# Attention trunk on one core: the input rows ahead of the weights, and a written-out order for the prologue

## The chip, the cores and the metric

The kernel runs on one NeuronCore of one Trainium2 chip, as one launch. The metric is device time in microseconds (us), the median over several executions. 0.2% of it is 3.0 us.

## The reference

A two-layer decoder trunk over 1040 tokens (16 learned meta tokens, then 1024 rows of x), width 1024, float32. Each layer does this:

```python
u = rms_norm(h, norm_g)
proj = jnp.einsum('bld,dp->blp', u, w_in)      # 4104 columns
dq, dk, dv, dz, fq, fk, fv, fz, f_logit = jnp.split(proj, split_points, axis=-1)
q1, q2 = diff_qk(dq); k1, k2 = diff_qk(dk)     # with rotary embedding
p = probs(qa, k1) - lam * probs(qc, k2)        # 4 differential heads, causal
...                                            # 8 forgetting heads with a decay term
mixed = jnp.concatenate([o_a * silu(dz), o_b * silu(fz)], axis=-1)
h = h + jnp.einsum('blm,md->bld', mixed, w_out)
```

After the second layer a last RMSNorm is applied and the meta tokens are dropped.

## The kernel before

Every large product is made of three matmuls: each operand is split into a high and a low part (`whi`, `wlo` for weights, `XTh`, `XTl` for the transposed input), and hi x hi, lo x hi and hi x lo are accumulated in PSUM.

**The prologue** (lines 947 to 996) makes `XTh` and `XTl` for layer 0. A few matmuls without use (`WARM = 20`, line 951, each run as two instructions) go first. Then x comes in as eight blocks of 128 rows (512 KB each), the meta tokens as a ninth block of 16 rows, and the norm's weights `gb` as a broadcast of 512 KB; all of them on SP's DMA queue (lines 956 to 964). With `W0 = 0` the loop also calls `load_w` right after its first block: the weights of the first key projection (128 columns, 512 KB, two DMAs of 256 KB) go out on ACT's DMA queue (`WQ0`, line 308), and POOL splits them (lines 325 and 328).

The nine blocks are normed in three groups of three (`GRPS`, line 969). For a group, ACT squares and sums each block (line 260), DVE makes the reciprocal roots of the three sums together (lines 235 to 248) and scales each block (line 271). Then `put_ut` (line 274) transposes each block on PE in two halves (line 286), ACT copies a half into `XTh` (line 296), and DVE subtracts to make `XTl` (line 297). The first group is block 0 (meta) with blocks 1 and 2; the key projection's first chunk of 272 tokens needs that group alone, the second chunk of 384 the second group, and the third chunk the third.

`prefetch(0, PF0)` with `PF0 = "qv"` then asks for the first query projection's weights (two DMAs of 256 KB on ACT's queue, `WQ1`) and for the value weights of units 0 and 1 together with the forget weights (`load_v01`, line 362). The rotary tables `cos` and `sin` follow (lines 999 and 1000).

**The projections** of unit 0 (`unit_proj`, line 482) are key, query and value in the text's order. `proj` (line 344) takes one chunk after the other: 24 matmuls over the eight pieces k of the contraction, then the evacuation. After the evacuation of chunk 1 the keys go through the rotary embedding (lines 509 to 514: four DMAs on SP, DVE, POOL, DVE).

**The rest** is eight units of attention in each layer, four differential and four forgetting; the next unit's projections are issued among the attention of the present one. A differential query block copies its low query part into one of `NQZ = 3` zeroed buffers on POOL (`low_queries`, line 673), from which PE reads (line 692).

**What sets the order.** The program is given to a planner (line 1182, `schedule_with_timeline_sim` and `auto_bufs`). It models a timeline, orders each engine's instructions (SP's and ACT's DMA issues too) by when each could be issued and how soon its result is due, and may so leave the order of the text. Each engine then runs its list in order. Where a pool has a number of buffers written out (`STB = 3` for the pool `stk` with the keys, queries and half of the prologue's rows), the planner keeps to it; where there is none (`bufs=None`), it chooses one that the memory has room for.

## Time and profile before

| | |
|---|---|
| median of 3 executions | 1485.57 us (1485.4 to 1487.66) |
| the profiled execution | 1487.34 us |
| its span, first to last instruction | 1485.6 us |
| PE busy with matmuls | 1416.9 us, 95% of the span |
| DVE, ACT, POOL busy | 958.7, 698.6, 619.2 us |
| mean granted TensorE clock | 0.983 |

PE is the TensorE, DVE the VectorE, ACT the ScalarE, POOL the GpSimd, and SP the engine that issues most DMAs; "PEld" is PE's weight load and "q" behind an engine's name its sequencer, which waits and issues. Times in rows are us from the start of the span. In a timeline, a row's two first numbers are the start and the length of a run of like instructions (xN says how many), and what stands in brackets is how long the engine sat idle before it and which event ended that. PEclk is the share of TensorE's full 2.4 GHz that was granted: 0.50 is 1.2 GHz.

### The profile page before, as it was taken

What the parts mean: (1) busy time and instruction counts of PE and PEld (TensorE: products, weight loads), DVE (VectorE), ACT (ScalarE), POOL (GpSimd) and SP (SyncE); (2) the same over time, 40 slices, a digit from 0 to 9 for tenths busy, and PEclk for the clock granted to TensorE, in tenths of its full rate; (3) what the DMA queues carried; (4) which work ended last, traced back from release to release, by engine and by line L of the source; (5) the groups of instructions that cost most, each with busy time, mean ns of one, the idle gap of its engine ahead of it and who ended that gap; (6) DMA issues with size and microseconds to landing.
All of it is one profiled execution on the core that took longest, in us unless ns stands there. A gap on an engine that the chain in (4) does not pass through costs nothing.

```text
span 1485.6 us, 26706 instructions
## 1 busy us (share of the span) xinstructions
PE 1416.9 (95%) x9262; PEld 1350.0 (91%) x9262; DVE 958.7 (65%) x2721; ACT 698.6 (47%) x1729; POOL 619.2 (42%) x1118
## 2 busy tenths in 40 slices
PE   4889989999999999999998989999999999999997
PEld 4888989999999999996888989899999999999886
DVE  4548796867765666655654678677757565655554
ACT  3335554545554555554323455444446455544511
POOL 2616463542435443654015345445424444445400
PEclk7999999999999999999999999999999999999999
DMA  9315240353324234358333142324331323253632
GB/s 193 74 30 73 39 93 16 65 62 69 71 49 71 61 56 82 82 152 200 114 110 75 29 60 48 68 47 64 53 87 29 82 44 80 55 118 91 228 109 91
DMA packets 112215, 119.63 MB, mean 81 GB/s; under 512 B 15376, under 2 KB 92816, under 8 KB 112080
## 3 DMA queue, kind: packets, MB, share of 16 engines
q1 hardware_dynamic: 104592, 104.09, 32.2%
q10 hardware_dynamic: 7488, 13.83, 4.7%
q8 instruction: 73, 1.20, 0.3%
q14 instruction: 62, 0.51, 0.1%
HBM read 70.92 MB, written 21.54 MB: 62 GB/s over the span
## 4 chain that ended last, share of the span: by engine, by line
PE 75%; DVE 7%; DMA 4%; ACT 2%; issue 2%; SPq 1%; POOL 1%; DVEq 0%; ACTq 0%; POOLq 0%
PE pj L352 36%; PE pss L1073 5%; PE pj L1073 5%; PE pss L690 4%; PE pss L692 4%; PE pt L865 4%; PE po L800 3%; PE pj L417 3%; PE po L799 2%; DMA sw<-raw 1%; SPq L137 1%; DVE E L696 1%; PE pt L1073 1%; DVE raw L511 1%; DMA mt<-ms 1%
## 5 line engine op out<-in xcount | busy, mean ns | idle before, releaser
L352 PE MATMUL pj<-XTh,whi 128*128 128x346 f32 (+5 forms) x1392 | 453.8, 328 | 5.0 <-ACT XTh L296 1.9
L352 PE MATMUL pj<-XTh,wlo 128*128 128x346 f32 (+5 forms) x1392 | 452.9, 326 | 1.2 <-POOL wlo L328 1.2
L352 PE MATMUL pj<-XTl,whi 128*128 128x346 f32 (+5 forms) x1392 | 451.8, 325 | 1.1 <-DVE XTl L297 1.1
L352 PEld LDWEIGHTS pj<-XTh,whi 128*128 128x128 f32 x1392 | 264.3, 190 | 9.0 <-POOL whi L325 1.9
L352 PEld LDWEIGHTS pj<-XTh,wlo 128*128 128x128 f32 x1392 | 265.1, 190 | 2.5 <-POOL wlo L328 1.8
L352 PEld LDWEIGHTS pj<-XTl,whi 128*128 128x128 f32 x1392 | 264.8, 190 | 2.3 <-DVE XTl L297 1.7
L696 DVE CUSTOM_DVE_ANT_0 E<-pss,cst 128x346 f32<-128x346 f32 (+6 forms) x384 | 212.0, 558 | 77.0 <-PE pss L692 61.7
L703 ACT ACTIVATE E<-E,cst 128x656 f32<-128x656 f32 (+3 forms) x192 | 172.5, 898 | 141.7 <-DVE cst L696 137.8
L328 POOL TENSOR_TENSOR wlo<-wraw,whi 128x256 fp32r<-128x256 f32 x232 | 182.1, 785 | 16.3 <-PE pt L760 1.3
L774 DVE TENSOR_TENSOR ptl<-pt,pth 128x512 fp32r<-128x512 f32 (+1 forms) x240 | 147.6, 633 | 34.8 <-ACT pth L773 30.7
L690 PE MATMUL pss<-k,qa 128*128 128x400 f32 (+7 forms) x448 | 152.8, 347 | 12.1 <-DVE cst L696 6.9
L773 ACT CAST pth<-pt 128x512 fp32r<-128x512 f32 (+1 forms) x240 | 123.3, 545 | 72.8 <-PE pt L865 30.9
L325 POOL TENSOR_SCALAR whi<-wraw 128x256 fp32r<-128x256 f32 x232 | 101.0, 436 | 116.4 <-DMA wraw<-in_w_in_dram 115.2
L720 POOL TENSOR_SCALAR E<-E,cst 128x400 f32<-128x400 f32 (+2 forms) x96 | 83.7, 873 | 138.2 <-DVE cst L719 127.2
L673 POOL TENSOR_SCALAR XTl<-ql 64x128 fp32r<-64x128 f32 x136 | 53.0, 396 | 151.3 <-PE pss L692 127.3
L690 PEld LDWEIGHTS pss<-k,qa 128*128 128x128 f32 x448 | 84.8, 190 | 16.9 <-DVE cst L696 9.7
L865 PE MATMUL pt<-cst,E 128*128 128x128 f32 x576 | 87.1, 273 | 0.3 <-DVE cst L762 0.3
L799 PE MATMUL po<-pth,V 128*128 128x256 f32 x320 | 82.7, 283 | 0.0
L800 PE MATMUL po<-ptl,V 128*128 128x256 f32 x320 | 82.3, 286 | 0.0
L512 POOL TENSOR_TENSOR sw<-sw,sin 128x694 f32<-128x694 f32 (+5 forms) x32 | 50.6, 1581 | 76.0 <-DMA sw<-raw 63.8
L692 PE MATMUL pss<-k,q 68*128 68x400 f32 (+6 forms) x224 | 71.7, 326 | 0.5 <-DMA qa<-qa 0.5
L692 PE MATMUL pss<-k,XTl 128*128 128x400 f32 (+6 forms) x224 | 71.5, 325 | 0.0
(303 smaller groups left out, 2944.3 us busy)
## 6 DMA issues: line engine op xcount, KB each, us to landing
wraw<-in_w_in_dram SPq DMA_DIRECT2D x244, 128.0 KB
hb<-in_x_dram SPq DMA_DIRECT2D x16, 512.0 KB
wor<-in_w_out_dram SPq DMA_DIRECT2D x64, 128.0 KB
ms<-OT SPq DMA_DIRECT2D x8, 520.0 KB
k<-k ACTq DMA_DIRECT2D x16, 260.0 KB
h<-hb SPq DMA_DIRECT2D x8, 512.0 KB
ms<-OT SPq DMA_DIRECT2D x8, 512.0 KB
hb<-h SPq DMA_DIRECT2D x8, 512.0 KB
```

The source lines that it names most:

```text
L328: nc.gpsimd.tensor_tensor(out=lo, in0=raw, in1=hi.bitcast(F32), op=ALU.subtract)
L352: nc.tensor.matmul(ps[:, :n], lhsT=w, rhs=xx[:, k, t0:t0 + n], start=(cnt == 0), stop=(cnt == 23))
L690: nc.tensor.matmul(ps[:, :nn], lhsT=U.Qa[m][:, t:t + P], rhs=U.K1[m][:, c0:c0 + nn], start=True, stop=False)
L692: nc.tensor.matmul(ps[:, :nn], lhsT=low[m], rhs=U.Kb[m][:, c0:c0 + nn], start=False, stop=True)
L696: nc.vector.tensor_tensor_reduce(out=E[:, c0:c0 + n], in0=ps[:, :n], in1=k, scale=-1.0, scalar=s[:, c - 1:c] if CHN and c else -NEG, op0=A ...
L703: nc.scalar.activation(E[:, :W], E[:, :W], AF.Exp, scale=-1.0, bias=lo, accum_out=s[:, 4:5])
L773: nc.scalar.copy(hi, ps)
L774: nc.vector.tensor_tensor(out=lo, in0=ps, in1=hi.bitcast(F32), op=ALU.subtract)
L799: nc.tensor.matmul(o[:, :256], lhsT=U.V[:, kb, hd, :], rhs=hi, start=False, stop=False)
L800: nc.tensor.matmul(o[:, :256], lhsT=U.V[:, kb, hd, :], rhs=lo, start=False, stop=last)
L865: nc.tensor.transpose(ps[:, (2 * a + b) * P:(2 * a + b + 1) * P], PP[:, k0:k0 + P], ident)
L1073: nc.tensor.matmul(ps, lhsT=xx[:, k, m0:m0 + P], rhs=wo[k][w][:, c], start=(k == 0 and i == 0), stop=(k == KT - 1 and i == 2))
```

## The change

The key weights are loaded after the ninth block (`W0 = 8`), on SP's queue instead of ACT's, in four DMAs of 128 KB instead of two of 256 KB. The query weights go to SP as well (four DMAs of 128 KB through the small `es` buffers), behind the key weights; the tables go behind them, and the value weights behind the tables. `tc.issue_after(ins)` queues what its block holds behind `ins` on the engine of `ins`. With it, the transposes of the first two groups are followed on PE by the key projection's first two chunks, made together: piece k for chunk 0, piece k for chunk 1, then piece k+1 (`both`). The third group's transposes are held back (`late_ut`) and queued behind that pair. The DVE work of the value weights and of `setup_scalars` is queued behind the third group's last subtraction. The useless matmuls ahead become 40 (`WARM`), the zeroed query buffers 2 (`NQZ`), and the pool `stk` has no written-out number of buffers (`STB = 0`).

```diff
--- before.py
+++ after.py
@@ -14,6 +14,9 @@
 F32R = mybir.dt.float32r
 BF16 = mybir.dt.bfloat16
 I32 = mybir.dt.int32
+PE = mybir.EngineType.PE
+SP = mybir.EngineType.SP
+DVE = mybir.EngineType.DVE
 AF = mybir.ActivationFunctionType
 ALU = mybir.AluOpType
 
@@ -36,7 +39,7 @@
 MW = 584
 AHEAD = 3
 XORD = (1, 0, 2, 3, 4, 5, 6, 7, 8)
-W0 = 0
+W0 = 8
 ON_POOL = ()
 SPL_POOL = ()
 GRPS = ((0, 1, 2), (3, 4, 5), (6, 7, 8))
@@ -49,8 +52,8 @@
 ENG = ('g','d')
 WLB = 6
 VPB = 0
-STB = 3
-NQZ = 3
+STB = 0
+NQZ = 2
 PMB = 4
 OTB = 2
 Q2B = 2
@@ -70,14 +73,14 @@
 PQ = 0
 SH = 0
 PP = ()
-WARM = 20
+WARM = 40
 CKB = (0,)
 KR = True
 PG = ()
 AQ = True
 AV = True
-WQ0 = True
-WQ1 = True
+WQ0 = False
+WQ1 = False
 CORD = (1, 0, 2, 3)
 PSB = (0, 0, 0, 0)
 Z_AT = {0: [0], 1: [1], 2: [2], 4: [3], 7: [4, 5, 6, 7]}
@@ -129,6 +132,10 @@
     ps_s = ctx.enter_context(tc.tile_pool(name="ps_s", bufs=PSB[1] or None, space=PS))
     ps_t = ps_s if SH == 1 else ctx.enter_context(tc.tile_pool(name="ps_t", bufs=PSB[2] or None, space=PS))
     ps_o = ps_t if SH == 2 else ctx.enter_context(tc.tile_pool(name="ps_o", bufs=PSB[3] or None, space=PS))
+
+    def last_of(engine):
+
+        return next(i for i in reversed(nc.cur_bb.bb.instructions) if i.engine == engine)
 
     def f32(ap):
         return ap.bitcast(F32) if ap.dtype == F32R else ap
@@ -304,8 +311,8 @@
         if rawroom == "half":
 
             whole = stk.tile([P, L], F32, name="wraw4", tag=rawtag, bufs=STB or None)[:, :D].rearrange("p (k c) -> p k c", k=KT)
-            for a in (0, 4):
-                (q or nc.sync).dma_start(out=whole[:, a:a + 4], in_=w_in[l, P * a:P * a + 4 * P, col:col + P].rearrange("(k p) c -> p k c", p=P))
+            for a in range(0, KT, 2):
+                (q or nc.sync).dma_start(out=whole[:, a:a + 2], in_=w_in[l, P * a:P * a + 2 * P, col:col + P].rearrange("(k p) c -> p k c", p=P))
             raws = [whole[:, 2 * qt:2 * qt + 2] for qt in range(4)]
         elif rawroom:
             for qt in range(4):
@@ -341,17 +348,29 @@
         while late:
             late.pop(0)()
 
-    def proj(l, col, chunks, evac):
+    def proj(l, col, chunks, evac, both=False):
         his, los = ahead.pop((l, col), None) or load_w(l, col)
+        def mms(ps, k, t0, n):
+            hi, lo = his[k // 2][:, k % 2, :], los[k // 2][:, k % 2, :]
+            for i, (w, xx) in enumerate(((hi, XTh), (lo, XTh), (hi, XTl))):
+                nc.tensor.matmul(ps[:, :n], lhsT=w, rhs=xx[:, k, t0:t0 + n],
+                                 start=(k == 0 and i == 0), stop=(k == KT - 1 and i == 2))
+
+        if both:
+
+            two = [pj(f"pj_{l}_{col}") for _ in range(2)]
+            with tc.issue_after(last_of(PE)):
+                for k in range(KT):
+                    for ps, (t0, n) in zip(two, chunks):
+                        mms(ps, k, t0, n)
+            for ps, (t0, n) in zip(two, chunks):
+                evac(ps, t0, n)
+            chunks = chunks[2:]
+            yield 0.0
         for t0, n in chunks:
             ps = pj(f"pj_{l}_{col}")
-            cnt = 0
             for k in range(KT):
-                hi, lo = his[k // 2][:, k % 2, :], los[k // 2][:, k % 2, :]
-                for w, xx in ((hi, XTh), (lo, XTh), (hi, XTl)):
-                    nc.tensor.matmul(ps[:, :n], lhsT=w, rhs=xx[:, k, t0:t0 + n],
-                                     start=(cnt == 0), stop=(cnt == 23))
-                    cnt += 1
+                mms(ps, k, t0, n)
             run_late()
             evac(ps, t0, n)
             yield 24 * n / 2370.0
@@ -488,7 +507,7 @@
         lowhalf, tophalf = slice(0, 64), slice(64, 128)
         halves = (lowhalf, tophalf)
 
-        def project(col, chunks, t_lo, scale, split):
+        def project(col, chunks, t_lo, scale, split, both=False):
 
             if not diff:
                 def ev(ps, t0, n):
@@ -512,7 +531,7 @@
                 nc.gpsimd.tensor_tensor(out=sw[:, c], in0=sw[:, c], in1=tabs[1][:, c], op=ALU.mult)
                 (nc.gpsimd if "a" in ENG else nc.vector).tensor_tensor(out=raw[:, c], in0=raw[:, c], in1=sw[:, c], op=ALU.add)
                 split(raw, a0, 1.0, a0, n)
-            yield from proj(l, col, chunks, ev)
+            yield from proj(l, col, chunks, ev, both)
 
         def sub(dst, src, scale, hi, which):
             if scale == 1.0:
@@ -536,7 +555,7 @@
                 hi = U.K1[m][halves[m], t0:t0 + n]
                 hi_part(hi, x, scale)
                 sub(U.K1[m][halves[1 - m], t0:t0 + n], x, scale, hi, f'k{m}')
-        yield from project(ck, CH_BLK if j in CKB else CH_ALL, 0, 1.0, split_k)
+        yield from project(ck, CH_BLK if j in CKB else CH_ALL, 0, 1.0, split_k, l == 0 and j == 0)
         if not diff and KE:
             U.Kb = []
             for m in range(2):
@@ -966,6 +985,7 @@
             ck0 = unit_cols(0)[1]
             ahead[0, ck0] = load_w(0, ck0, nc.scalar if WQ0 else None, None, "half", "qa0")
     utags = ("k0", "k1", "qa0", "qa1") * 2 + ("ql",)
+    late_ut = []
     for grp in GRPS:
         us = [stk.tile([P, L], F32, name="u", tag=utags[b])[:, :D] for b in grp]
         rs = rms_stats([hbs[b] for b in grp], us, nc.gpsimd if RP else nc.vector)
@@ -976,7 +996,11 @@
                 put_ut(b, u, r=r)
             else:
                 rms_apply(*hbs[b], r, gb, u, on_pool=b in ON_POOL)
-                put_ut(b, u, b in SPL_POOL)
+                if grp is GRPS[-1]:
+                    late_ut.append((b, u))
+                else:
+                    put_ut(b, u, b in SPL_POOL)
+
     def prefetch(l, todo):
 
         for w in todo:
@@ -985,26 +1009,38 @@
                 ahead[l, col] = load_w(l, col)
             if w == "q":
                 room = vp.tile([P, NB, 2, P], F32R, name="wroom", tag="V")
-                if l == 0:
-                    ahead[l, col] = load_w(l, col, nc.scalar if WQ1 else None, room, "half", "qa1")
-                else:
-                    ahead[l, col] = load_w(l, col, None, room,
-                                           lambda qt: slot("es")[:, :256].rearrange("p (k c) -> p k c", k=2))
+                ahead[l, col] = load_w(l, col, None, room,
+                                       lambda qt: slot("es")[:, :256].rearrange("p (k c) -> p k c", k=2))
             if w == "v":
                 ahead[l, "v"] = load_v01(l)
 
-    prefetch(0, PF0)
+    with tc.issue_after(last_of(SP)):
+        prefetch(0, "q")
     for l in range(DEPTH):
         tabs = (q2t("cos", F32), q2t("sin", F32))
-        dma(tabs[0], cos_t)
-        dma(tabs[1], sin_t)
+        with tc.issue_after(last_of(SP)):
+            dma(tabs[0], cos_t)
+            dma(tabs[1], sin_t)
+        tables = last_of(SP)
         units = [Unit() for _ in range(8)]
         tq = 0 if l == 0 else NM
         if (l, "v") not in ahead and not VLATE:
             ahead[l, "v"] = load_v01(l)
-        drain(unit_proj(l, 0, units[0], tabs))
+        g = unit_proj(l, 0, units[0], tabs)
         if l == 0:
-            setup_scalars()
+
+            next(g)
+            with tc.issue_after(last_of(PE)):
+                for b, u in late_ut:
+                    put_ut(b, u)
+
+            split = last_of(DVE)
+            with tc.issue_after(split), tc.issue_after(tables):
+                prefetch(0, "v")
+        drain(g)
+        if l == 0:
+            with tc.issue_after(split):
+                setup_scalars()
         for j in range(8):
             run_late()
             drain(attend(units[j]))
```

## Rows read from the trace of the kernel before

**Rows 1.** The page's first part: busy us, share of the span, instructions.
```profile
PE 1416.9 (95%) x9262; PEld 1350.0 (91%) x9262; DVE 958.7 (65%) x2721; ACT 698.6 (47%) x1729; POOL 619.2 (42%) x1118
```

**Rows 2.** Busy time by stretch; columns as the first line says.
```profile
core 0: us, PE busy (x) PEld busy (x) DVE busy (x) ACT busy (x) POOL busy (x), PEclk, DMA share, GB/s
0.00:31.00 31.00, 11.03 (x64) 10.33 (x64) 8.73 (x36) 14.04 (x28) 8.55 (x25) 0.72 0.93 190
31.00:52.00 21.00, 16.35 (x96) 15.12 (x96) 16.98 (x32) 6.97 (x14) 15.13 (x24) 0.84 0.62 115
...
100.00:200.00 100.00, 93.52 (x614) 89.28 (x613) 80.50 (x239) 53.54 (x138) 51.06 (x90) 0.98 0.34 56
800.00:900.00 100.00, 90.49 (x625) 87.99 (x624) 70.02 (x198) 48.05 (x122) 37.71 (x72) 0.97 0.26 41
```

**Rows 3.** The timeline of PE, 24 to 81 us.
```profile
26.05 3.67 PE L286 MATMUL pt<-cst,u 128*128 128x128 f32 x16 [0.16 <-DVE u L271]
31.06 0.36 PE L352 MATMUL pj<-XTh,whi 128*128 128x272 f32 x1 [1.33 <-ACT XTh L296]
...
33.28 0.42 PE L352 MATMUL pj<-XTh,whi 128*128 128x272 f32 x1
...
36.45 0.40 PE L352 MATMUL pj<-XTl,whi 128*128 128x272 f32 x1
...
50.42 1.47 PE L286 MATMUL pt<-cst,u 128*128 128x128 f32 x12
...
75.61 0.28 PE L417 MATMUL pj<-vwh,XTl 128*128 128x264 f32 x1
79.78 0.25 PE L810 MATMUL pss<-k,qa 128*128 128x16 f32 x1 [3.89 <-ACT V L421]
```

**Rows 4.** The timeline of DVE, 20 to 60 us.
```profile
21.36 0.17 DVE L261 TENSOR_SCALAR cst<-cst 128x3 f32<-128x3 f32 x1 [20.18 <-ACT u L260]
...
23.53 3.66 DVE L271 SCALAR_TENSOR_TENSOR u<-hb,cst,gb 16x1024 f32<-16x1024 f32 x3
...
38.43 3.81 DVE L271 SCALAR_TENSOR_TENSOR u<-hb,cst,gb 128x1024 f32<-128x1024 f32 x3
42.17 4.86 DVE L297 TENSOR_TENSOR XTl<-pt,XTh 128x512 fp32r<-128x512 f32 x8
```

**Rows 5.** The timeline of ACT, 0 to 20 us.
```profile
4.94 1.06 ACT L260 ACTIVATE u<-hb 128x1024 f32<-128x1024 f32 x1 [1.57 <-DMA hb<-in_x_dram]
5.90 0.19 ACT L260 ACTIVATION_READ_ACCUMULATOR u<-hb 128x1 f32 x1
18.03 1.06 ACT L260 ACTIVATE u<-hb 16x1024 f32<-16x1024 f32 x1 [11.94 <-DMA hb<-in_meta_tokens_dram]
```

**Rows 6.** The timeline of SP's DMA issues, 0 to 20 us.
```profile
0.80 0.87 SPq L137 DMA_DIRECT2D hb<-in_x_dram  x2
...
8.22 9.81 SPq L137 DMA_DIRECT2D hb<-in_x_dram  x5
```

**Rows 7.** Four more stretches, for DMA: share of the 16 engines, GB/s.
```profile
5.00:10.00 5.00, 3.91 (x31) 3.72 (x30) 0.00 (x0) 1.09 (x2) 0.00 (x0) 1.00 1.03 73
18.00:25.00 7.00, 0.14 (x2) 0.14 (x2) 3.25 (x13) 6.33 (x11) 1.91 (x4) 0.50 1.02 407
...
690.00:694.00 4.00, 4.00 (x19) 2.91 (x18) 0.00 (x0) 0.00 (x0) 2.18 (x5) 1.00 1.02 53
43.00:46.00 3.00, 2.71 (x12) 2.21 (x13) 3.00 (x6) 1.17 (x2) 3.00 (x7) 0.58 0.85 158
```

**Rows 8.** POOL's groups by line, 0 to 52 us, and one timeline row.
```profile
L325 POOL TENSOR_SCALAR wroom<-wraw 128x256 fp32r<-128x256 f32 x4 | 4.1, 1044 | 5.5 <-DMA wraw<-in_w_in_dram 5.5
L328 POOL TENSOR_TENSOR wroom<-wraw,wroom 128x256 fp32r<-128x256 f32 x4 | 2.9, 731 | 0.0
...
17.76 0.78 POOL L325 TENSOR_SCALAR whi<-wraw 128x256 fp32r<-128x256 f32 x2 [4.39 <-DMA wraw<-in_w_in_dram]
```

**Rows 9.** The page's groups, of POOL's query copies in the whole span.
```profile
L673 POOL TENSOR_SCALAR XTl<-ql 64x128 fp32r<-64x128 f32 x136 | 53.0, 396 | 151.3 <-PE pss L692 127.3
```

## Prediction

> **What bounds the kernel now.** I read the page's busy times first: PE has 1416.9 us of a span of 1485.6 [rows 1], so nothing that leaves PE's work alone can win more than 68.7 us, and the question is where PE stands idle. The busy times by stretch answer it [rows 2]. From 0 to 31 us PE is busy for 11.0 us, most of it the useless matmuls; from 31 to 52 it is busy for 16.4 of 21 at a mean granted clock of 0.84. The next largest gaps are in the differential units, 6.5 us in 100 to 200 and 9.5 in 800 to 900. So the prologue is the one stretch in which PE waits long, and behind it PE is nearly always busy: what the prologue ends earlier, the whole program should end earlier.
>
> Then I followed the prologue back. PE's first useful product starts at 31.06 us and its second key chunk ends at 50.4, where a run of 12 transposes begins [rows 3]. DVE, which both need, sat idle for 20.2 us until 21.36 and waited for ACT's sums [rows 4]. ACT had its first block at 4.94 us and then waited 11.9 us for the 16 meta rows, until 18.03 [rows 5]. SP issued the first two x blocks at 0.80, but spent 9.81 us from 8.22 on to issue five more [rows 6]. The DMA engines say why: from 5 to 10 us they were fully busy (share 1.03) and moved 73 GB/s; from 18 to 25, with x alone, the same share moved 407 [rows 7]. The 73 falls where the key weights were under way: POOL waited for their second half until 17.76 [rows 8]. Layer 1 shows the same for the first weights it touches: 53 GB/s at a share of 1.02. Later weight rows of a layer go faster (158 GB/s, share 0.85) [rows 7]. So the first weights of a layer hold all DMA engines for some 10 us, and in the kernel before these 10 us lie ahead of x.
>
> **The change part by part.**
>
> *x ahead of the weights.* I take it that x1, x2 and the meta rows are issued first, since their sums are due earliest. Block 1 lands as now, at 4.94; 0.59 MB more at 407 GB/s is 1.4 us, so ACT squares three blocks without a wait: 4.94 + 3 x 1.25 [rows 5] = 8.7 us. DVE starts there in place of 21.36: 12.7 us earlier. If gb and one more block go in between (2 x 0.52 MB / 407 = 2.6 us) it is 11.3; above 12.7 there is nothing, as block 1 can't land earlier.
>
> *DVE up to the pair.* For a group it has 23.53 - 21.36 = 2.2 us of roots and 3.7 to 3.8 of scaling [rows 4]. The subtractions of two groups are 10 halves of 4.86 / 8 = 0.61 and two small ones of the meta block, which I count as one more: 6.7 us. So two groups take 2 x (2.2 + 3.7) + 6.7 = 18.5 us, to 27.2. The other end: the planner puts the third group's roots and scaling (6.0 us) ahead, as it does now, where the scaling at 38.43 stands before the eight subtractions at 42.17 [rows 4]; that gives 33.2. I take 28.0, near the lower end, because the third group is now due only behind the pair; 0.8 is for small operations in between.
>
> *The key weights behind x.* x, gb and meta are 4.78 MB; with 0.52 landed at 4.94, the other 4.26 at 407 GB/s end at 15.4. Then 0.52 MB at 73 to 53 GB/s [rows 7] takes 7.2 to 9.9 us: 22.6 to 25.3. POOL needs 1.04 + 0.73 = 1.8 us a piece beside a busy DVE [rows 8], so the last of four pieces is ready at 24.4 to 27.1, and earlier ones earlier. Weights and XTl come at about the same time; DVE covers the weights until 28.0. If that cover goes, little changes: three quarters of the pair (7.4 us) run ahead of the last piece, which is needed at 35.4 only, 8 us after its worst time here.
>
> *The pair.* It has 24 matmuls of 272 columns and 24 of 384. At the lower clock 14 steps of 272 take 36.45 - 33.28 = 3.17 us [rows 3], 0.226 each and 0.32 for 384: 13.1 us in all. At the full clock it is half: 6.6. PE has only scattered transposes ahead of it, and with little to do from 18 to 25 us its granted clock was 0.50 [rows 7]; but the useless matmuls and the transposes may lift it, so I take the middle, 9.8 us. The pair ends at 37.8; the second chunk ends at 50.4 now: 12.6 us gained. The order by pieces itself changes no count of matmuls.
>
> *The third group.* At 50.4 us 12 of its 24 transposes are still to come (1.47 us for 12 [rows 3]); in the changed kernel all 24 are: 1.5 us lost. Its six subtractions (3.7 us) end about 4.4 us after the pair, while PE has 2.9 us of transposes; the first half of the query projection could fill the rest, but the list may put the third key chunk first. I take 0.9 lost (bounds 0 and 1.5). Its roots and scaling fit between 28.0 and 37.8 on DVE.
>
> *What moves on SP and POOL.* The queue holds, behind the key weights (25.3 us), query weights of 0.52 MB at 158 GB/s (3.3 us), tables of 1.06 MB at 407 (2.6) and value weights of 1.05 MB (6.6): about 28.6, 31.2 and 37.9 us. The tables are first needed behind the pair's evacuation (37.8), the query weights with 4 x 1.8 us of POOL by 36, and the value weights with 8 x 1.8 by some 52, where query and keys end. What hides them is the pair and 17 us of projections; without that cover each counts in full. ACT loses four DMA issues, which wait on nothing; I count zero. The 128 KB pieces come from SP, which has nothing else due then.
>
> *40 useless matmuls.* The first 20 ran from 2.59 us on; 6.3 us for them and at most as much again ends at 15.2, while the first transposes are ready at about 12.2. DVE has the second group's roots and scaling (to 20.5) before it needs them. Zero.
>
> *Two query buffers and an open `stk` pool.* No wait of PE in the trace is for the query copies; POOL waits for PE there [rows 9]. Lower bound zero, with no gain, as a buffer less frees nothing; upper bound in the rivals. An open pool may shift the planner's order anywhere, in both directions; I take zero.
>
> **Sum.** 12.6 - 1.5 - 0.9 = 10.2 us. The stall of 3.9 us before 79.78 [rows 3], where the first attention waits in PE's list, I leave as it is. The profiled execution took 1487.3, 1.8 above the median; 1487.3 - 10.2 is 1477.1, and by the median **1475.4**. With the best ends (27.2 and 6.6) the gain is 15.1, 1470.5; with the worst (33.2, 13.1, both losses) 1.1, 1484.5, but both worst ends together are unlikely: this case's own range is 1470 to 1483.
>
> **Rivals.**
>
> *The clock stays low (1481).* In the kernel before, matmuls that stood back to back from 33.28 to 36.45 us ran at half rate though PE had been busy, and 16 transposes from 26.05 on took 3.67 us, 0.23 each against 1.47 / 12 = 0.12 later [rows 3]. If the new prologue leaves PE so many short waits that the clock stays at 1.2 GHz until the third group is through, the pair takes 13.1 and not 9.8, and the 24 transposes 5.5 and not 2.9: 5.9 us less gain, 1475.4 + 5.9 = 1481.3. For it: DVE feeds PE in small pieces. Against it: the mean grant from 31 to 52 us was 0.84 [rows 2], nearer to full. The Trainium skill, page "TensorE: Matmul & The Clock Gate", section "HAM oscillation — how this bites in real kernels", speaks for this case: bursts of matmuls that are parted by waits for their operands fall back to the slow clock each time and pay for it each time. By that rule the time would be this rival's; the trace agrees in part, with 0.50 while PE had little to do and 0.84 in the broken stretch behind.
>
> *The change does not do what it says (1486).* `W0 = 8` moves a call in the text only; the planner orders SP's issues by its own due times. If it puts the key weights ahead of the second group's rows, DVE starts early but then waits for them, and the 7 to 10 us come back: 1483 to 1488. Against it: the rows' path to the pair (sum, roots, scaling, transpose, subtraction) is much longer than that of the weights.
>
> *POOL held by two query buffers (1491).* This one ends slower. POOL already stands 127 us in 41 waits for PE before a query copy [rows 9]. With two buffers the copy for block i+2 waits for block i and not for the one before; all POOL work behind it (the next unit's weight splits, the rotary products) comes later, and PE waits for that. It happens in the differential units alone, where PE is now idle for 6.5 and 9.5 us of a hundred [rows 2]. If that idle time doubled, 16.0 us would be lost: 1475.4 + 16.0 = 1491.4. It turns the sign from 13.2 us on. For it: POOL's waits are long. Against it: no PE wait ends at that copy now.
>
> *More than I count (1469).* If the planner's new list also fills the 3.9 us stall at 75.7, and the lower clock behind it goes, some 6 us more are won.
>
> **How the numbers follow.** Forecast 0.60, low clock 0.13, not what it says 0.08, two buffers 0.12, more 0.07. About 0.2%, 3.0 us, is what a measurement can tell from no change: faster means below 1482.6. Faster gets nearly all of the forecast (0.58), most of the clock case (0.11) and all of the last (0.07), and a little of the third: 0.77. Slower is the buffers and a little of the third: 0.13. Same: 0.10. The range of 8 in 10 takes in the forecast, the clock case and half of the case above: 1466 to 1484.
>
> **What would show it.** Right: DVE's first root near 9 us, x landed near 15 at some 400 GB/s, then a stretch of 50 to 75 GB/s at a full DMA share; the pair between 28 and 38; transposes behind it; the first attention near 69 in place of 79.8; from 100 us on the same busy shares. Wrong: DVE still starting near 20 (the order of x), the pair at 0.226 us a step to its end (the clock), or PE's idle time in 100 to 300 and 800 to 1000 growing by more than 13 us (the buffers).

## The result, and the profile after

The changed kernel takes 1477.3 us (median of 4 runs, 1474.76 to 1480.28) against 1486.62 for the kernel before (median of 4 runs, 1485.4 to 1491.08). The ratio on record is 0.9923, 95% interval 0.9896 to 0.9951; the two medians alone divide to 0.9937, inside it. The profiled execution took 1479.28 us, its span is 1477.5, 8.1 less than before. The forecast was 1475.4, so number and sign came out. The way there did not: the prologue won three quarters of what was forecast, layer 0 gave back more than that, and the gain that was measured was made in layer 1, where I had expected nothing.

The page's busy line and the group of the query copies, against [rows 1, 9]:

```profile
PE 1425.7 (96%) x9302; PEld 1353.0 (92%) x9302; DVE 974.1 (66%) x2721; ACT 696.1 (47%) x1729; POOL 629.8 (43%) x1118
...
L692 POOL TENSOR_SCALAR XTl<-ql 64x128 fp32r<-64x128 f32 x136 | 54.3, 401 | 185.2 <-PE pss L711 137.3
```

The same stretches as in [rows 2], and 200 to 300 and 600 to 700 us besides:

```profile
0.00:31.00 31.00, 22.28 (x147) 21.66 (x147) 20.40 (x55) 17.44 (x34) 10.17 (x24) 0.89 0.93 220
31.00:52.00 21.00, 16.45 (x102) 16.19 (x103) 11.89 (x18) 5.74 (x11) 13.61 (x16) 0.92 0.31 52
...
100.00:200.00 100.00, 90.36 (x583) 84.32 (x583) 84.89 (x218) 51.86 (x132) 59.76 (x96) 0.98 0.42 66
200.00:300.00 100.00, 92.56 (x603) 87.91 (x603) 70.30 (x192) 46.56 (x120) 44.35 (x80) 0.97 0.33 53
...
600.00:700.00 100.00, 95.81 (x581) 84.91 (x580) 63.51 (x168) 55.38 (x142) 56.45 (x94) 0.98 0.57 149
...
800.00:900.00 100.00, 96.73 (x675) 94.54 (x674) 71.11 (x202) 48.42 (x125) 42.63 (x75) 0.97 0.28 45
```

Two of these stretches of the kernel before have not been shown yet:

```profile
200.00:300.00 100.00, 94.49 (x648) 90.77 (x647) 79.45 (x210) 52.25 (x133) 49.87 (x87) 1.00 0.29 56
600.00:700.00 100.00, 98.33 (x600) 89.00 (x600) 56.92 (x131) 50.16 (x121) 57.09 (x94) 1.00 0.60 155
```

So from 100 to 200, 200 to 300 and 600 to 700 us PE does 31, 45 and 19 matmuls fewer than before; from 800 to 900 it does 50 more. Next the prologue. PE's timeline of the changed kernel, against [rows 3]:

```profile
21.88 5.38 PE L293 MATMUL pt<-cst,u 128*128 128x128 f32 x24 [5.40 <-DVE u L278]
26.91 0.57 PE L356 MATMUL pj<-XTh,whi 128*128 128x272 f32 x1
...
29.77 0.29 PE L356 MATMUL pj<-XTh,whi 128*128 128x272 f32 x1
35.10 0.60 PE L356 MATMUL pj<-XTh,wlo 128*128 128x272 f32 x1 [5.04 <-POOL wlo L335]
...
36.26 0.75 PE L356 MATMUL pj<-XTh,wlo 128*128 128x384 f32 x2
...
41.40 2.78 PE L293 MATMUL pt<-cst,u 128*128 128x128 f32 x24
44.63 0.44 PE L356 MATMUL pj<-XTh,whi 128*128 128x384 f32 x1 [0.45 <-ACT XTh L303]
...
60.32 0.28 PE L415 MATMUL pj<-vwh,mm 128*48 128x264 f32 x1
...
85.50 0.28 PE L436 MATMUL pj<-vwh,XTl 128*128 128x264 f32 x1
85.62 0.17 PE L829 MATMUL pss<-k,qa 128*128 128x16 f32 x1
```

The pair does not run as the text has it. All 19 matmuls from 26.91 to 29.77 are of chunk 0 (272 columns), and 22 of its 24 stand ahead of the first of chunk 1 (384 columns): the planner kept the pair behind the transposes, but not the order by pieces inside it.

DVE's timeline, against [rows 4]:

```profile
8.85 0.17 DVE L268 TENSOR_SCALAR cst<-cst 128x3 f32<-128x3 f32 x1 [7.67 <-ACT u L267]
...
28.93 0.68 DVE L304 TENSOR_TENSOR XTl<-pt,XTh 128x512 fp32r<-128x512 f32 x1
```

POOL's timeline shows where the 5.04 us come from: the last low half of the key weights stands behind copies of query weights that wait for their transfer.

```profile
30.89 2.49 POOL L332 TENSOR_SCALAR wroom<-cst 128x256 fp32r<-128x256 f32 x2 [1.90 <-DMA cst<-in_w_in_dram]
33.34 1.70 POOL L335 TENSOR_TENSOR wlo<-wraw,whi 128x256 fp32r<-128x256 f32 x1
```

Two stretches for the DMA, against [rows 7]: x, then the key weights behind it.

```profile
10.00:14.00 4.00, 4.00 (x37) 3.88 (x36) 3.79 (x9) 1.47 (x3) 0.00 (x0) 1.00 1.03 420
...
15.00:21.00 6.00, 1.48 (x14) 1.24 (x12) 4.79 (x18) 5.59 (x13) 0.40 (x1) 1.00 1.06 65
```

**Where the 8.1 us came from.** Two rows of PE's timeline cut every run in three: the first matmul of the value projection (67.98 before, 60.32 after), and the matmul right behind layer 1's last transposes, which is here called the start of layer 1. Before, with the wait inside layer 1 that will matter:

```profile
780.71 0.44 PE L352 MATMUL pj<-XTh,whi 128*128 128x384 f32 x1 [0.24 <-ACT XTh L296]
808.08 0.67 PE L690 MATMUL pss<-k,qa 128*128 128x400 f32 x1 [3.85 <-DMA qa<-qa]
```

After, where no such wait follows:

```profile
784.37 0.44 PE L356 MATMUL pj<-XTh,whi 128*128 128x384 f32 x1 [0.24 <-ACT XTh L303]
```

These cuts split equal work: 4441 matmuls lie behind the start of layer 1 in every run, and 4565 between the two cuts (the rows below count one or two more, which are still running at a cut). To the value projection 7.7 us are won. From there to layer 1 the kernel before takes 780.71 - 67.98 = 712.7 us and the changed one 784.37 - 60.32 = 724.1: 11.3 lost. From there to the end it is 1485.6 - 780.71 = 704.9 against 693.1: 11.8 won. The three make 8.1. The busy times of the two layers, before and then after, say how much of this is waiting:

```profile
67.98:780.71 712.73, 694.93 (x4566) 658.59 (x4565) 478.43 (x1383) 345.04 (x884) 298.71 (x544) 1.00 0.38 79
780.71:1485.60 704.89, 678.82 (x4441) 650.23 (x4441) 447.12 (x1263) 328.05 (x797) 286.49 (x517) 0.99 0.34 77
```

```profile
60.32:784.37 724.05, 701.95 (x4567) 660.07 (x4565) 482.48 (x1385) 344.85 (x886) 306.43 (x552) 0.99 0.37 78
784.37:1477.50 693.13, 676.72 (x4441) 646.79 (x4441) 457.34 (x1263) 327.06 (x797) 293.22 (x518) 0.99 0.35 78
```

In layer 0 PE is idle for 22.1 us instead of 17.8, and busy for 7.0 us more with the same matmuls. In layer 1 it is idle for 16.4 us instead of 26.1, and busy for 2.1 us less.

One difference in PE's list is plain in both layers. The kernel before puts the first scores of unit 0 into the middle of the value projection, and PE waits there: 3.85 us before 808.08 for the queries' transfer, and 3.89 us before 79.78, where the row names ACT's copy of values [rows 3] (the same wait in d_nqz below, 3.99 us before 81.13, is put down to the queries' transfer). The changed kernel puts them behind it, and does not wait.

### The profile page after: what moved, and what is told of

The parts are those of the page before. It is cut to its first block, busy times and chain, and to the rows that moved or that the text cites. A ratio compares the mean times of both kernels' runs of the same rounds, so it can differ in the third digit from the quotient of the medians.

```text
span 1477.5 us, 26876 instructions
## 1 busy us (share of the span) xinstructions
PE 1425.7 (96%) x9302; PEld 1353.0 (92%) x9302; DVE 974.1 (66%) x2721; ACT 696.1 (47%) x1729; POOL 629.8 (43%) x1118
## 4 chain that ended last, share of the span: by engine, by line
PE 70%; DVE 5%; DMA 3%; ACT 2%; issue 1%; SPq 1%; POOL 1%; DVEq 0%; ACTq 0%
PE pj L356 33%; PE pss L1109 6%; PE pj L1109 5%; PE pt L884 3%; PE pss L709 3%; PE pss L711 3%; PE po L819 2%; PE po L818 2%; PE pj L436 2%; PE pt L1109 2%; DVE E L715 1%; SPq L144 1%; DMA wraw<-in_w_in_dram 1%; PE po L816 1%; DMA mt<-ms 1%
## 5 line engine op out<-in xcount | busy, mean ns | idle before, releaser
L715 DVE CUSTOM_DVE_ANT_0 E<-pss,cst 128x456 f32<-128x456 f32 (+6 forms) x384 | 211.8, 557 | 79.8 <-PE pss L711 61.9
L722 ACT ACTIVATE E<-E,cst 128x400 f32<-128x400 f32 (+2 forms) x192 | 172.4, 898 | 138.7 <-DVE cst L715 125.8
L332 POOL TENSOR_SCALAR whi<-wraw 128x256 fp32r<-128x256 f32 x232 | 106.9, 461 | 110.6 <-DMA wraw<-in_w_in_dram 85.4
L692 POOL TENSOR_SCALAR XTl<-ql 64x128 fp32r<-64x128 f32 x136 | 54.3, 401 | 185.2 <-PE pss L711 137.3
L884 PEld LDWEIGHTS pt<-cst,E 128*128 128x128 f32 x576 | 68.0, 141 | 7.5 <-DVE cst L715 4.2
```

What stands on the lines that cost most here:

```text
L715: nc.vector.tensor_tensor_reduce(out=E[:, c0:c0 + n], in0=ps[:, :n], in1=k, scale=-1.0, scalar=s[:, c - 1:c] if CHN and c else -NEG, op0=A ...
L722: nc.scalar.activation(E[:, :W], E[:, :W], AF.Exp, scale=-1.0, bias=lo, accum_out=s[:, 4:5])
L884: nc.tensor.transpose(ps[:, (2 * a + b) * P:(2 * a + b + 1) * P], PP[:, k0:k0 + P], ident)
```

## The experiments

All runs in one table; the kernel before is measured again beside each. "v" is the first matmul of the value projection, "L1" the start of layer 1, both from PE's timeline; layer 0 is L1 - v, layer 1 is span - L1. The last column says where PE's list has unit 0's first scores in layer 1: in the middle of the value projection or behind it. All in us. The kernel before took 1486.62 beside the changed kernel and 1488.45 to 1489.21 beside the later runs, so totals that were taken apart are best compared by their ratios.

| run | v | L1 | layer 0 | layer 1 | span | median | ratio to before | scores |
|---|---|---|---|---|---|---|---|---|
| before | 67.98 | 780.71 | 712.7 | 704.9 | 1485.6 | 1486.62 | 1 | middle |
| after | 60.32 | 784.37 | 724.1 | 693.1 | 1477.5 | 1477.30 | 0.9923 (0.9896 to 0.9951) | behind |
| f_pool | 61.19 | 786.41 | 725.2 | 707.7 | 1494.1 | 1495.79 | 1.0045 (1.0024 to 1.0065) | middle |
| e_w0 | 70.05 | 794.49 | 724.4 | 708.1 | 1502.6 | 1503.80 | 1.0094 (1.0066 to 1.0122) | middle |
| b_nqz3 | 62.77 | 785.58 | 722.8 | 704.1 | 1489.7 | 1490.88 | 1.0004 (0.9987 to 1.0022) | middle |
| d_bufsonly | 69.07 | 788.97 | 719.9 | 688.2 | 1477.2 | 1478.87 | 0.9930 (0.9910 to 0.9950) | behind |
| n_w39 | 56.42 | 781.52 | 725.1 | 708.0 | 1489.5 | 1491.37 | 1.0014 (0.9999 to 1.0029) | middle |
| d_nqz | 69.23 | 787.10 | 717.9 | 701.0 | 1488.1 | 1487.77 | 0.9999 (0.9983 to 1.0015) | middle |
| vf1_before | 69.17 | 785.17 | 716.0 | 696.0 | 1481.2 | 1481.06 | 0.9949 (0.9932 to 0.9967) | behind |
| vf_nqz3 | 61.30 | 770.33 | 709.0 | 695.6 | 1465.9 | 1470.62 | 0.9874 (0.9853 to 0.9895) | behind |
| p_old | 68.81 | 780.81 | 712.0 | 692.3 | 1473.1 | 1476.35 | 0.9911 (0.9884 to 0.9938) | behind |
| x_old | 68.39 | 808.53 | 740.1 | 692.6 | 1501.1 | 1507.81 | 1.0127 (1.0092 to 1.0162) | behind |
| vf_warm20 | 56.05 | 784.12 | 728.1 | 692.2 | 1476.3 | 1478.83 | 0.9927 (0.9899 to 0.9955) | behind |
| vf_pool | 61.20 | 770.43 | 709.2 | 697.0 | 1467.4 | 1470.59 | 0.9872 (0.9844 to 0.9900) | behind |

Where two runs share PE's list to the last instruction, apart from the useless matmuls ahead, they share their layer times: f_pool, e_w0 and n_w39 (layer 0 from 724.4 to 725.2, layer 1 from 707.7 to 708.1), and vf_nqz3 and vf_pool (709.0 and 709.2, 695.6 and 697.0). So the 14 runs are 11 different lists.

**1. GpSimd's order in the prologue (f_pool).**

```diff
-    with tc.issue_after(last_of(SP)):
+    with tc.issue_after(last_of(SP)), tc.issue_after(last_of(POOL)):
         prefetch(0, "q")
```

> The changed kernel, with the query weights' first pieces ordered behind the last split of the key weights on GpSimd too. Theory 1 (GpSimd's in-order list made the 5.04 us stall of TensorE at 35.1 us: the last key weights' low half stood behind query weight copies that waited for their transfer): the stall falls under 1 us, the value projection of layer 0 ends some 5 us earlier (near 81 us in place of 86), and the run takes about 1472 us if the rest keeps its course. Theory 2 (the stall only hides another lateness, the third group's rows): the stall moves to the third group's transposes and the value projection ends within 2 us of 86. Theory 3 (every edit makes the planner write another order of the later stages): the prologue gains what theory 1 says, and the whole run may still end anywhere between 1465 and 1482 us.

The stall went, but DVE was late in its place (PE's timeline):

```profile
24.59 4.34 PE L294 MATMUL pt<-cst,u 128*128 128x128 f32 x24 [8.22 <-DVE u L279]
...
35.74 0.69 PE L357 MATMUL pj<-XTl,whi 128*128 128x384 f32 x1 [3.44 <-DVE XTl L305]
...
76.71 0.35 PE L830 MATMUL pss<-k,qa 128*128 128x16 f32 x1 [7.58 <-DMA qa<-qa]
```

DVE's timeline shows why the 3.44 us stand there: the third group's scaling is ahead of the last subtractions that the pair needs.

```profile
30.47 4.62 DVE L279 SCALAR_TENSOR_TENSOR u<-hb,cst,gb 128x1024 f32<-128x1024 f32 x3
35.01 1.27 DVE L305 TENSOR_TENSOR XTl<-pt,XTh 128x512 fp32r<-128x512 f32 x2
```

The value projection starts 0.9 us later than in the changed kernel. That is nearer to theory 2, but the wait is for the second group's rows and not the third's, and DVE's list moved along with POOL's, so the run does not price the stall by itself. No theory foresaw the total, 18.5 us over the changed kernel: the scores are back in the middle of the value projection, with a wait of 7.58 us, and layer 1 takes 707.7.

**2. The key weights back among x (e_w0).**

```diff
-W0 = 8
+W0 = 0
```

> The changed kernel with the key weights' four loads back among the loads of x on SyncE's queue, and the written-out order of the prologue kept. Theory 1 (the order of the loads carries the gain): VectorE still starts near 8.9 us, but the second group's rows come some 5 to 8 us later, TensorE's second set of transposes moves from 21.9 to about 25 to 28 us, and the value projection of layer 0 ends 3 to 8 us later than in the changed kernel. Theory 2 (the written-out order carries it, and the rows of x wait for VectorE anyway): the value projection ends within 2 us of the changed kernel's 86 us, or earlier, since the key weights' low halves are ready sooner and the 5.04 us stall goes.

PE's second set of transposes moved further than theory 1 said, to 37.86:

```profile
37.86 5.38 PE L293 MATMUL pt<-cst,u 128*128 128x128 f32 x24 [17.50 <-DVE u L278]
```

The value projection starts 9.7 us later than in the changed kernel and 8.9 later than in f_pool. With f_pool this run shares PE's list to the last instruction, and is 8.0 us slower in the median; but f_pool has the order on POOL besides. n_w39 (run 4) has the same list too, without that order and with one useless matmul fewer: against it the value projection starts 13.6 us later and the ratio is 0.8% higher, some 12 us. So x ahead of the weights is worth 8 to 14 us where PE's list stays as it is, and all or nearly all of it lasts to the end.

**3. Three query buffers in the changed kernel, and the buffers alone in the kernel before (b_nqz3, d_bufsonly).**

```diff
-NQZ = 2      # b_nqz3, from after.py
+NQZ = 3
```

> The changed kernel with three query buffers in place of two (the number of before). Theory 1 (two buffers cost layer 0 its 18 us): from the end of the value projection to the end of layer 0 the time returns to that of before, layer 0 ends near 766 us in place of 784, GpSimd waits less in front of its query copies (137 us in the changed kernel), and the run takes 1462 to 1467 us. Theory 2 (the planner's new order of the later stages is what cost layer 0 its time, and the buffers do nothing): layer 0's end stays within 10 us of 784 with no gain to be seen, and the run takes 1470 to 1485 us.

```diff
-STB = 3      # d_bufsonly, from before.py
-NQZ = 3
+STB = 0
+NQZ = 2
```

> The kernel before with only the changed kernel's numbers of buffers (two query buffers, the key stack's buffers left to the allocator), its order of loads and prologue kept. Theory 1 (the buffers cost layer 0 its 18 us): the value projection of layer 0 ends near 100 us as before, layer 0 ends some 15 to 20 us later than before's 780 us, and the run takes 1495 to 1505 us. Theory 2 (the buffers do nothing, the order of the later stages is what moves): the run takes 1480 to 1493 us, with layer 0's end within 7 us of 780.

The buffers do not cost layer 0 its time: with three it still takes 722.8. Both totals lie outside what either theory gave, the first above and the second below. The new prologue with three buffers wins nothing (1.0004), and the buffers alone, with the old prologue, win all that the change wins (0.9930). The last column orders the runs so far, and that made the list theory of the next runs: the gain hangs on where the list has the first scores, and any edit may move them.

**4. One useless matmul fewer (n_w39).**

```diff
-WARM = 40
+WARM = 39
```

> The changed kernel with one useless matmul fewer ahead (WARM 39 for 40), and nothing else. The planner then writes another list: TensorE's has layer 0's first scores ahead of the second half of the value projection, as in the kernel before; in the changed kernel the whole value projection stands ahead of them, in layer 0 and (but for the meta block's) in layer 1. List theory (where those scores stand is worth some 10 us, and the changed kernel's gain over the kernel before is this): TensorE waits 7 to 8 us for the first scores near 78 us, layer 1 takes 704 to 709 us as in the three runs with that list, not 693.6, and the run takes 1487 to 1494 us. Prologue theory (the gain comes from the prologue, and the list's order is of no weight): 1475 to 1480 us.

The list theory holds: 1491.37 in place of 1477.30, from one matmul that nothing uses. The prologue was even better (the value projection starts at 56.42, with neither the stall of the changed kernel nor the late subtractions of run 1), but the two waits are back:

```profile
72.46 0.35 PE L829 MATMUL pss<-k,qa 128*128 128x16 f32 x1 [8.10 <-DMA qa<-qa]
...
809.68 0.67 PE L709 MATMUL pss<-k,qa 128*128 128x400 f32 x1 [4.65 <-DMA qa<-qa]
```

**5. Two query buffers alone in the kernel before (d_nqz).**

```diff
-NQZ = 3
+NQZ = 2
```

> The kernel before with two query buffers in place of three, and nothing else. Its list for TensorE keeps the first scores ahead of half of the value projection in both layers, as in the kernel before. List theory: no gain, 1484 to 1494 us. Buffer theory (two buffers as such make the run faster, as they seemed to where the key stack's buffers were left open too, 1478.9 us): 1475 to 1481 us.

No gain, no loss (0.9999), with the scores in the middle as before. So two buffers as such are worth nothing either way; in d_bufsonly it was, by the last column, the list that they and the open pool brought about together (the open pool alone, without a written-out order, was not run).

**6. The order alone, in layer 1 of the kernel before (vf1_before).**

```diff
+            if j == 0 and l == 1:
+                with tc.issue_after(last_of(PE)):
+                    drain(attend(units[j]))
+            else:
                 drain(attend(units[j]))
```

> The kernel before with one order written out: in layer 1 unit 0's attention is queued on TensorE behind the whole value projection. Layer 0 and the prologue keep their text. List theory: TensorE's wait of 3.85 us before 808.1 us goes, layer 1 takes some 693 us in place of 705, and the run takes 1473 to 1480 us, as much as the changed kernel without any of its prologue. Rival (the later list has other differences that bring the gain in layer 1, not this one): within 4 us of the kernel before's 1489.

1481.06, 1 us above the range of the list theory and well away from the rival. Layer 1 takes 696.0 in place of 704.9; the wait is gone, and PE is busy for 96.71 us from 800 to 900 instead of 90.49 [rows 2]:

```profile
800.00:900.00 100.00, 96.71 (x687) 93.88 (x686) 72.22 (x205) 49.91 (x128) 42.57 (x77) 1.00 0.28 45
```

So one order, with nothing of the prologue, brings two thirds of the change's gain. It wins 8.9 us in layer 1, more than the 3.85 of the wait itself; the rest of the list is new here too. Over all 14 runs layer 1 takes 688.2 to 697.0 with the scores behind and 701.0 to 708.1 with them in the middle.

**7. The order in both layers, three buffers, new prologue (vf_nqz3).**

```diff
-NQZ = 2
+NQZ = 3
...
+            if j == 0:
+                with tc.issue_after(last_of(PE)):
+                    drain(attend(units[j]))
+            else:
                 drain(attend(units[j]))
```

> The changed kernel with three query buffers and, in both layers, unit 0's attention queued on TensorE behind the whole value projection (with three buffers alone it took 1490.9 us, with the first scores ahead of half of the value projection). List theory: the wait of 7.75 us before 78.5 us and that of 4.98 us before 814 go, layer 1 takes some 693 us in place of 704.6, and the run takes 1470 to 1480 us. Rival (two buffers bring the gain): 1486 to 1494 us.

As the list theory said, and better than both kernels: 1470.62, ratio 0.9874. Here layer 0 keeps the prologue's lead: layer 1 starts 10.4 us earlier than before.

```profile
61.30 0.28 PE L415 MATMUL pj<-vwh,mm 128*48 128x264 f32 x1
...
770.33 0.44 PE L356 MATMUL pj<-XTh,whi 128*128 128x384 f32 x1 [0.24 <-ACT XTh L303]
```

**8. The old prologue under the same order (p_old).**

The kernel before with `STB = 0` and the edit of run 7 but its buffers.

```diff
-STB = 3
+STB = 0
...
+            if j == 0:
+                with tc.issue_after(last_of(PE)):
+                    drain(attend(units[j]))
+            else:
                 drain(attend(units[j]))
```

> The kernel before with its own prologue, loads and three query buffers, the key stack's buffers left open, and the same written-out order as the run before it (vf_nqz3, 1470.6 us): unit 0's attention behind the whole value projection, in both layers. What is left between the two is the prologue with its loads. Prologue theory (under a fixed order the prologue's lead of 10 to 12 us, which vf_nqz3 has from 80 us to layer 0's end, lasts to the end of the run): 1479 to 1485 us. Rival (layer 0 takes such a lead back, as in the changed kernel, where 13 us at 90 us had become a loss of 3.7 by 784): 1468 to 1475 us.

1476.35, between the two ranges. Beside it in the same session vf_pool (run 11, the new prologue) took 1468.9 to 1472.49 against p_old's 1474.86 to 1478.05: under a written-out order the new prologue's kernel is 5.8 us faster by the medians. These are one list each, and the next runs show how far the list alone can move the time under this same order (run 10 has the new prologue and is slower than p_old), so 5.8 is not yet the prologue's own worth. In the traces of p_old and vf_nqz3 its lead is 7.5 us at the value projection, 10.5 at layer 1 and 7.2 at the end.

**9. x behind weights under that order (x_old).**

```diff
-W0 = 8       # from vf_nqz3
+W0 = 0
```

> vf_nqz3 with the key weights' loads back among those of x. Theory 1 (x ahead of all weights is the part of the prologue that pays, as e_w0 and f_pool, which have one and the same list for TensorE and are 8.0 us apart, say): TensorE waits some 17 us before its second set of transposes near 38 us, and the run takes 1476 to 1482 us, that is, all or most of what p_old loses to vf_nqz3. Rival (the later list has slack enough that 8 us at 50 us come back): 1468 to 1474 us.

Both theories failed. The prologue went the way of theory 1 (PE waits 11.51 us, of 17 expected, and the value projection starts 7.1 us later), but then layer 0 took 740.1 us in place of 709.0. The written-out order pins one place of the list, and the rest still moves.

**10. 20 useless matmuls under that order (vf_warm20).**

```diff
-WARM = 40    # from vf_nqz3
+WARM = 20
```

> vf_nqz3 with 20 useless matmuls ahead in place of 40. Theory 1 (with the order written out the run no longer hangs on small edits, and the 20 more are worth nothing, as predicted): 1467 to 1474 us. Rival 1 (they hold the clock up for the transposes and the pair): the transposes from 26 us and the pair run longer, 1473 to 1478 us. Rival 2 (the rest of the list still jumps with any edit): off by more than 5 us to either side, with the first 60 us as before.

Rival 2 for the larger part: the prologue ends 5.2 us earlier, but layer 0 takes 728.1, and the run 8.2 us more. The 20 more do hold the clock up for a while: the first group's 24 transposes took 2.56 us in vf_nqz3 and 1.03 + 3.68 here, and the 24 before the pair 4.73 and 5.38. But PE waits for DVE between the two sets, 10.12 us there and 6.58 here, and the value projection starts later there all the same.

**11. GpSimd's order under that order (vf_pool).**

The edit of run 1, on vf_nqz3.

> vf_nqz3 with the query weights' first pieces queued behind the key weights' last split on GpSimd too (the edit of f_pool). TensorE's list is the same as in vf_nqz3. Theory 1 (what ends the prologue's waits is VectorE, 10.1 us before the second set of transposes and 2.8 before the third chunk's low half, so that GpSimd's order is of no weight): 1468 to 1473 us. Rival (GpSimd's splits beside VectorE are still late for the pair): 2 to 4 us less, 1466 to 1469 us.

Theory 1: 1470.59 against 1470.62. With PE's list the same, POOL's order is of no weight here: the waits ahead of the third group's transposes, 12.19 and 1.25 us, both end with DVE.

## Why the prediction came out right, and where it was wrong

By its own steps:

- *x ahead of the weights: right.* DVE starts at 8.85 (forecast 8.7). x is in by 15 us at 420 GB/s, then the weights come at 65. Run 2 prices the move at 8 to 14 us with PE's list unchanged.
- *DVE up to the pair: nearly.* The last subtraction of two groups ends at 28.93 + 0.68 = 29.6 (forecast 28.0, bounds 27.2 to 33.2).
- *The key weights behind x: wrong.* The last piece was to be ready at 27.1 at the latest and "needed at 35.4 only". PE needed its low half at 35.10 - 5.04 = 30.06, and POOL had it ready at 33.34 + 1.70 = 35.04. Two steps of the prediction failed here. It had three quarters of the pair running ahead of the last piece; PE's list ran 19 of 48 matmuls, for the order by pieces was not kept. And the step "what moves on SP and POOL" asked when each transfer lands, not what stands behind it in POOL's list: query weights stand ahead of that low half, wait 1.90 us for their transfer and take 2.49 us. In run 4 POOL has the same order there, but the same two steps take 0.82 and 0.74 us in place of 2.49 and 1.70; its pair also begins later, at 30.10, and PE has no such wait. Why the steps are slower here was not tried. Run 4 starts the value projection 3.9 us earlier than the changed kernel, so most of the 5.04 can be won; run 1 loses it again to DVE's list.
- *The pair: right in size.* 26.91 to 41.40 less 5.04 is 9.45 us (forecast 9.8). It ends at 41.4, not 37.8, for the stall. *The third group:* 2.78 us of transposes and 0.45 of wait, as counted. In all 7.7 us are won at the value projection, of 10.2 forecast.
- *Two query buffers: right.* Run 5 leaves them at zero, and the rival falls: POOL waits 137.3 us for PE in the changed kernel (140.3 in run 5) where it waited 127.3, and PE does not notice (0.9999 in run 5). *40 useless matmuls: zero by themselves, not through the list.* The clock that they hold up is lost in waits for DVE (run 10), but one of them fewer brings another list, and with it 14 us (run 4).
- *The stall of 3.9 us "I leave as it is", and "from 100 us on the same busy shares": wrong.* The stall is gone in both layers, layer 0 takes 11.3 us more and layer 1 11.8 less.

The step that failed is the sentence on the open pool: "may shift the planner's order anywhere, in both directions; I take zero". As a mean it may be zero. As a bound it was missing: runs 4 and 9 put 14 us (the total) and 31 us (layer 0) on it, several times the sum that I worked out with care, and the range of 1466 to 1484 held by luck as much as by working. The planner writes the whole program's list anew for every edit. In this change the new list took the prologue's gain in layer 0 and gave another in layer 1. One matmul fewer (run 4), and the same prologue would have measured 0.14% slower than before, within what can be told from no change.

How layer 0 loses its time is seen in part. From 240 to 300 us the waits of PE in the changed kernel, grouped by who ends them:

```profile
PE pss L709 <- DVE cst L715: 4.3, 4, 1.9
PE pt L884 <- DVE cst L678: 1.3, 1, 1.3
```

and in the kernel before:

```profile
PE po L797 <- DVE ptl L774: 0.8, 1, 0.8
```

PE waits there for DVE's minimum over each block of scores; as I read it, too little other work stands between. Why the planner leaves so little there was not found: it is not the number of query buffers (run 3), and with the new prologue and no written-out place for the scores layer 0 takes 722.8 to 725.2 us in all five runs (three different lists), wherever the scores stand, against 712.7 to 719.9 with the old one.

The clock is the other part. Where these waits lie, the granted clock falls to the lower level in the changed kernel and stays full in the kernel before:

```profile
274.00:280.00 6.00, 4.12 (x16) 3.72 (x15) 5.91 (x11) 4.68 (x9) 4.65 (x9) 0.50 0.58 167
```

```profile
274.00:280.00 6.00, 5.89 (x40) 5.61 (x40) 4.86 (x11) 2.92 (x8) 1.71 (x4) 1.00 0.00 0
```

The same happens at 195.5 to 198.5 and 660 to 662.5 us (0.50 in both); in its layer 0 the kernel before has such stretches at 81.2 to 84.4, behind its wait for the scores, and at 129 to 132 only. That goes with the 7.0 us of longer busy time; how much of them the clock explains was not separated.

The clock rival did not come in the prologue, but its mechanism shows there once: behind the 5.04 us stall the granted clock is 0.50 from 35 to 38 us, and the pair's steps take twice as long. The Trainium skill, page "TensorE: Matmul & The Clock Gate", section "HAM oscillation — how this bites in real kernels", has it that bursts parted by waits fall back to the slow clock; the trace agrees there, and 24 transposes at 41.40 took 2.78 us, the full rate, where those at 21.88 took 5.38.

## What to carry to other kernels

Where a planner orders the whole program, cut both traces at the same two or three instructions and compare stretch by stretch: a total, even one that comes out as forecast, says little about the part that was edited. Before a gain of 1% is believed, make an edit that should do nothing and see how far the time moves; here one unused matmul moved it by 14 us. And write out the orders that matter: putting the first scores behind the value projection, one `issue_after`, took the new prologue with three query buffers from 1.0004 to 0.9874 of before. One written-out place does not hold the rest, though (runs 9 and 10): look in the trace whether the list is the one that was meant, as the pair's order by pieces here was not.

## What was not expected of the hardware

The key weights are as slow behind x as they were ahead of it: 65 GB/s at a DMA share of 1.06, on SP's queue in pieces of 128 KB, where x just before had 420 GB/s at 1.03. Before, on ACT's queue in pieces of 256 KB and with x beside them, it was 73 [rows 7]. So with queue, piece size and company all changed at once, the rate stayed where it was; none of the three was changed alone, and what makes these first weights slow was not tried.
